# An added 16-row load at the head of SyncE's queue in an add-and-GELU kernel

## The chip, the cores and the metric

The kernel runs on one core of a Trainium2 chip. The metric is the device time of one execution in microseconds; lower is better. Before the change it is 120.06 us (median of three runs, 120.06 to 120.14). All times given as positions ("at 31.45") are microseconds from the start of the profiled span.

## The reference

```python
batch, dim = 1024, 4096          # x and y: float32

def reference(x, y):
    z = x + y
    return (0.5 * z * (1 + np.tanh(np.sqrt(2 / np.pi) * (z + 0.044715 * z ** 3)))).astype(np.float32)
```

It is an elementwise add followed by GELU in its tanh form. Two arrays of 16.78 MB are read and one of 16.78 MB is written; nothing is used twice.

## The kernel before

**Tiling.** Each array is viewed as 128 partitions by 32768 elements; a partition's row is 128 KB of consecutive memory. One tile `z` holds a whole array (128 x 32768). x is loaded straight into it, y is added to it, and the result is written over it and stored from it. y goes through two buffers of 8192 columns each (`YS`), used in turn.

**Transfers.** All are issued by SyncE, in the order of the list `sp` (line 173): y0, x0, y1, x1, y2, y3, and then three stores. A y load has 8192 columns (4 MB in all, 32 KB per partition), an x load 16384 (8 MB), and the stores have 16384, 10240 and 6144. The loads y2 and y3 take over the buffers of y0 and y1, so each waits until the adds that read the old content are done (`needs`, line 183). The first store also waits for the first part of chunk 8's last step (`FIRST`, line 98), so that stores join the queue shortly before the loads end.

**Compute.** The columns are worked on in 16 chunks of 2048 (`CH`). For each chunk: `add` (z += y, on VectorE for six chunks and on GpSimd for ten, table `by_dve`), `mag` (ScalarE writes the absolute value of z into a PSUM tile w), `gelu` (ScalarE applies GELU to -w in place), and `end` (VectorE writes max(z, 0) + w back to z). This uses that GELU(z) is max(z, 0) plus GELU of minus the absolute value of z.

**Order.** Each engine has a list of its own (`sp`, `pool`, `acts`, `dve`). The loop at line 199 emits from each list whatever has its needs emitted already, and the schedule is kept as emitted. What an instruction really waits for at run time are semaphores that the framework derives from the tiles that it reads and writes.

**Head and tail.** `begin_early` (line 9) runs on the finished program: it takes the first `count` transfers of SyncE out of the body, checks that they wait for nothing, and puts them at the front of the program's head, before the start-up work and the barrier that ends it. It is called with a count of 2 (line 214), so y0 and x0 are issued there. `wait_late` (line 23) takes the wait for the last store out of the closing sequence and puts it at the very end, on ScalarE, so that the closing barriers and semaphore clearing run while the last stores are under way.

Of the kernel before, what the change touches and what calls it, by code (L numbers as in the profile page):

```python
# [66 lines left out]
def kernel(  # L67
# [14 lines left out]
    nc = tc.nc  # L82
    P = nc.NUM_PARTITIONS
    fp32 = mybir.dt.float32
# [6 lines left out]
    xv, yv, ov = (a.rearrange("(p n) d -> p (n d)", p=P) for a in (x, y, out))  # L91
# [22 lines left out]
    pool_sb = ctx.enter_context(tc.tile_pool(name="xz", bufs=1))  # L114
# [55 lines left out]
            ends.setdefault(c, ins.ins)  # L170


    sp = [(load_y, 0), (load_x, 0), (load_y, 1), (load_x, 1), (load_y, 2), (load_y, 3)]
    sp += [(store, i) for i in range(len(stores))]
    pool = [(add, c) for c in range(C) if c not in by_dve]
    dve, acts = [], []
    for c in range(C):
        dve += [(add, k) for k in sorted(by_dve) if by_dve[k] == c] + [(end, c)]
        acts += [(mag, c), (gelu, c)]

    needs = {
        load_x: lambda i: [],
        load_y: lambda i: [
            (add, c) for c in over(cr, yr[i][0] - 2 * YS, yr[i][1] - 2 * YS)
# [61 lines left out]
```

## Time and profile before

| what | us |
|---|---|
| median of three runs | 120.06 |
| profiled span, first to last instruction | 118.57 |
| VectorE busy | 59.8 |
| ScalarE busy | 60.8 |
| GpSimd busy | 55.5 |
| last landing of y0 (issued at 0.00) | 12.01 |
| last landing of x0 (issued at 0.43) | 31.35 |
| last landing of y3 | 79.86 |
| first store issued | 77.61 |
| last store issued | 107.56 |
| last landing of the last store | 118.53 |

The profiled execution is one run of its own; its span counts from the first instruction to the last, and the median of the runs lies 1.49 us above it.

How to read it: "busy" counts compute instructions; an instruction that only starts a transfer shows with its engine's queue (SPq for SyncE), and the transfer itself is carried by 16 DMA engines that work next to each other. Each packet of a transfer (here one partition's row) has a record with its start and duration. A load has landed when all 16 engines have reported on its semaphore. The rows and stretches themselves are shown with the prediction.

### The profile page before, as it was taken

Reading aid. Unit: us, or ns where it says so; the run is one execution under the profiler, and the core shown is the slowest. Engines: PE = TensorE matmul, PEld = TensorE weight load, DVE = VectorE, ACT = ScalarE, POOL = GpSimd, SP = SyncE. Lnnn points to the kernel's source line nnn. Section 1 sums busy time; section 2 is a strip of 40 time slices with the busy share of each in tenths; the row PEclk is TensorE's granted clock in tenths of the full one; section 3 lists DMA queues with packets and bytes.
Section 4 is the critical chain, followed back from the end, with each engine's and each line's share of the span. In section 5 each row is a group of like instructions: output and inputs, shape, how many; then the busy total and the mean of one; then the engine's idle time right before and its main releaser. Section 6 shows DMA issues by size and latency. Waiting matters only on the chain.

```text
span 118.6 us, 160 instructions
## 1 busy us (share of the span) xinstructions
DVE 59.8 (50%) x24; ACT 60.8 (51%) x34; POOL 55.5 (47%) x14
## 2 busy tenths in 40 slices
DVE  0000000000399999699994594257999457742000
ACT  5000000000067979999379705797798999940000
POOL 0000000000399999997000029999999999100000
DMA  7989888998889988988899898998899889999996
GB/s 243 464 365 696 354 354 354 663 398 354 354 387 497 531 354 354 707 354 354 354 420 464 365 520 354 531 531 354 354 531 531 354 354 442 442 442 442 398 398 265
DMA packets 1296, 50.33 MB, mean 424 GB/s; under 512 B 144, under 2 KB 144, under 8 KB 144
## 3 DMA queue, kind: packets, MB, share of 16 engines
q1 hardware_dynamic: 1296, 50.33, 98.6%
HBM read 33.55 MB, written 16.78 MB: 424 GB/s over the span
## 4 chain that ended last, share of the span: by engine, by line
DMA 48%; POOL 34%; POOLq 4%; ACT 3%; DVE 2%; issue 0%; SPq 0%; DVEq 0%
POOL z L149 34%; DMA z<-in_x_dram 26%; DMA y<-in_y_dram 21%; POOLq L213 4%; DVE z L166 2%; ACT w L154 2%; ACT w L157 2%; SPq L132 0%; POOLq L149 0%; DVEq L166 0%
## 5 line engine op out<-in xcount | busy, mean ns | idle before, releaser
L149 POOL TENSOR_TENSOR z<-z,y 128x2048 f32<-128x2048 f32 x10 | 55.3, 5563 | 45.6 <-DMA z<-in_x_dram 31.1
L154 ACT ACTIVATE w<-z 128x2048 f32<-128x2048 f32 x16 | 30.1, 1880 | 42.5 <-DVE z L149 36.0
L166 DVE SCALAR_TENSOR_TENSOR z<-z,w 128x2048 f32<-128x2048 f32 (+1 forms) x17 | 36.4, 2157 | 16.0 <-ACT w L157 16.0
L149 DVE TENSOR_TENSOR z<-z,y 128x2048 f32<-128x2048 f32 x6 | 24.0, 4009 | 30.3 <-DMA z<-in_x_dram 30.1
L157 ACT ACTIVATE w<-w 128x2048 f32<-128x2048 f32 x16 | 29.8, 1862 | 0.5
L198 ACT ACT_TABLE_LOAD x1 | 1.3, 1283 | 1.3 <-PEq L230 1.3
L197 DVE MEMSET one<- 128x1 f32 x1 | 0.1, 59 | 1.3 <-PEq L230 1.3
L198 ACT ACTIVATE one<-one 128x1 f32<-128x1 f32 x1 | 0.2, 203 | 0.0
L230 POOL MEMSET const-float32-0.0<- 128x1 f32 x1 | 0.1, 98 | 0.2 <-issue 0.2
L230 POOL MEMSET const-bfloat16-1.0<- 128x1 bf16 x1 | 0.1, 101 | 0.0
L230 POOL MEMSET const-uint8-127<- 128x1 uint8 x1 | 0.1, 101 | 0.0
L230 POOL MEMSET const-float32-1.0<- 128x1 f32 x1 | 0.1, 98 | 0.0
## 6 DMA issues: line engine op xcount, KB each, us to landing
y<-in_y_dram SPq DMA_DIRECT2D x4, 4096.0 KB, 23.7
out_dram<-z SPq DMA_DIRECT2D x1, 5120.0 KB, 14.9
out_dram<-z SPq DMA_DIRECT2D x1, 3072.0 KB, 11.0
z<-in_x_dram SPq DMA_DIRECT2D x2, 44.9
out_dram<-z SPq DMA_DIRECT2D x1, 21.6
```

Source lines behind the costliest of these rows:

```text
L149: eng.tensor_add(out=zt[:, a:b], in0=zt[:, a:b], in1=yt[s][:, o : o + b - a])
L154: nc.scalar.activation(out=wt[c], in_=zt[:, a:b], func=act.Abs)
L157: nc.scalar.activation(out=wt[c], in_=wt[c], func=act.Gelu_apprx_tanh, scale=-1.0)
L166: ins = nc.vector.scalar_tensor_tensor(out=zt[:, a + o : a + o + n], in0=zt[:, a + o : a + o + n], scalar=0.0, in1=wt[c][:, o : o + n], op ...
L197: nc.vector.memset(one, 0.0)
L198: nc.scalar.activation(out=one, in_=one, func=act.Gelu_apprx_tanh)
L213: tc.compile()
L230: nc = _bacc.Bacc("TRN2", target_bir_lowering=False, num_devices=1)
```

## The change

A further entry, `first`, stands at the head of SyncE's list. It allocates a tile of its own, `tiny`, of 128 x 128 float32 (512 B per partition) in the pool that holds `z`, and loads 16 rows of 128 elements of y into it, 512 B each, 8 KB in all. Nothing reads that tile. It has no needs. All else, the count of 2 given to `begin_early` among it, is as before.

```diff
-    sp = [(load_y, 0), (load_x, 0), (load_y, 1), (load_x, 1), (load_y, 2), (load_y, 3)]
+    def first(_):
+        tiny = pool_sb.tile([P, 128], fp32, tag="tiny", name="tiny")
+        nc.sync.dma_start(out=tiny[:16], in_=yv[:16, :128])
+
+    sp = [(first, 0), (load_y, 0), (load_x, 0), (load_y, 1), (load_x, 1), (load_y, 2), (load_y, 3)]
     sp += [(store, i) for i in range(len(stores))]
...
     needs = {
+        first: lambda i: [],
         load_x: lambda i: [],
```

## The prediction

> **What bounds the kernel now.** I first read the page's utilisation rows: is any engine, or the memory traffic, full from end to end?
>
> ```profile
> span 118.6 us, 160 instructions
> DVE 59.8 (50%) x24; ACT 60.8 (51%) x34; POOL 55.5 (47%) x14
> ...
> DMA packets 1296, 50.33 MB, mean 424 GB/s; under 512 B 144, under 2 KB 144, under 8 KB 144
> q1 hardware_dynamic: 1296, 50.33, 98.6%
> ```
>
> No compute engine is busy for more than half of the span; the 16 DMA engines have a packet in hand for 98.6% of it. The chain of waits says something else at first sight:
>
> ```profile
> DMA 48%; POOL 34%; POOLq 4%; ACT 3%; DVE 2%; issue 0%; SPq 0%; DVEq 0%
> ```
>
> The 34% on POOL are adds that run while the queue still has transfers in it: the chain follows back from the last compute instruction, which ends at 107.5, while data flow until 118. So I asked next where in the span the traffic is not full, in stretches (the last two columns are the busy share of the DMA engines and GB/s; a packet counts in the stretch in which it starts, hence shares a little over 1):
>
> ```profile
> 0.00:1.00 1.00, 0.00 (x0) 0.00 (x0) 0.20 (x4) 1.00 0.00 0
> 1.00:4.00 3.00, 0.06 (x1) 1.49 (x2) 0.00 (x0) 1.00 0.98 360
> 4.00:40.00 36.00, 8.55 (x2) 5.61 (x3) 8.51 (x2) 1.00 1.01 436
> 40.00:80.00 40.00, 30.49 (x14) 30.76 (x18) 25.45 (x5) 1.00 1.03 446
> 80.00:116.00 36.00, 20.73 (x8) 22.97 (x13) 21.34 (x5) 1.00 0.96 416
> 116.00:118.60 2.60, 0.00 (x0) 0.00 (x0) 0.00 (x0) 1.00 0.66 284
> ```
>
> Between 4 and 116 us there is no hole. I strung the trace's packet records into 16 chains, one per DMA engine: none has an idle gap over 25 ns, at the seams between the nine transfers either. Each chain carries 3.146 MB, and a 32 KB packet takes 1.21 us (27.1 GB/s; 16 engines 433 GB/s), so a chain needs 3.146 MB / 27.1 GB/s = 116.1 us. The last packets end at 117.75 to 118.07, the last landing is at 118.53, and the span ends at 118.57. So **the time is the moment at which data start to flow, plus 116.1, plus 0.5 of landing**. Only the first term can move, apart from bytes. It stands here:
>
> ```profile
> 0.00 0.38 SPq L132 DMA_DIRECT2D y<-in_y_dram  x1
> 0.43 0.42 SPq L125 DMA_DIRECT2D z<-in_x_dram  x1
> 1.26 0.33 SPq L132 DMA_DIRECT2D y<-in_y_dram  x1
> 1.64 0.45 SPq L125 DMA_DIRECT2D z<-in_x_dram  x1
> ```
>
> SyncE begins the issue of y0 at 0.00 and ends it at 0.38. The packet records begin 0.64 later: the 16 engines' first packets start at 1.02, one after another, the last at 1.95. They take 2.14 us (earliest starter) down to 1.21 (the two latest), against 1.21 for any later packet, and end at 2.77 to 3.17. Taking 1.21 off each end gives the moment at which each engine flows: 1.56 to 1.95.
>
> **The change, part by part.**
>
> *The new issue on SyncE.* One issue of a kind with the four y loads, whose rows show 0.33 to 0.38 us. It is now the first instruction, so it should take the 0.38; y0's issue then starts at 0.43, as x0's does now, and takes 0.33. It ends at 0.76 instead of 0.38: **+0.38 us** on the path, with nothing in front of it to hide it.
>
> *What the DMA engines do with it.* 16 rows of 512 B are 8 KB, against 50.33 MB. If each engine gets one row, that is 512 B / 27.1 GB/s = 0.02 us, and a completion record of 9 ns (the duration of each of the 144 four-byte packets): 0.03 us per engine. These lie in the 0.38 by which y0 comes later, so I count nothing; if that cover is gone, 0.03. If one engine gets all the rows it is 0.3 us on that engine, which would outlast the cover only if the small transfer were itself late.
>
> *The latency of a first transfer.* The trace shows one start from idle and no second, so it does not say whether a small transfer in front takes over part of the start-up of y0. Bounds from the rows: y0's packets can start 0.64 after its issue ends, at 0.76 + 0.64 = 1.40, instead of 1.02. At best all 16 flow at once from 1.40: the last engine gains 1.95 - 1.40 = 0.55. At worst the writing out of a transfer over the 16 engines takes the 0.93 us between first and last start (1.95 - 1.02) whatever its size, and y0's begins behind the small one's: +0.93. I take the spread as it is, shifted by 0.38, because the two engines that start last (1.90 and 1.95) run their first packet at full rate, 1.21: what they wait for is their turn, not data, and they are among the latest to flow, so their turn sets the end.
>
> *What the change moves.* The helper that lifts transfers to the front of the program takes the first two SyncE transfers. Those are now the small load and y0; x0 stays behind in the body. The body's first issue is at 1.26 now, so x0 is issued at about 1.26, y1 at 1.26 + 0.42 + 0.05 = 1.73 and x1 near 2.1. None is needed before y0's last packet ends (the chains show 11.6). I cost this at nothing; the 9.7 us of y0's own packets hide it, and without that cover x0's delay, 1.26 - 0.43 = 0.83, would be paid in full.
>
> *Completion counters.* The landing records show eight counters for nine transfers, y0's used again by the last store. With ten, the last two stores use the small load's and y0's, which have long landed when the stores are issued. The final wait follows the last store's counter; clearing the others may take one more GpSimd instruction, near 112 us, behind which there are 6 us of stores. Nothing.
>
> *What is late next.* Adds, activations and ends follow the landings, so they shift with the stream. The tightest seam is the first store: issued at 77.61 when y3's last landing is at 79.86. It hangs on y2's landing, which shifts by the same amount, so the 2.2 us stay. The last store is issued at 107.56 with the store before it landing at 111.26: 3.7 us.
>
> **Rule against row.** The Trainium skill, "DMA: Bandwidth & Descriptors", in "Rules for kernel authors", speaks against the change: a transfer under 64 KB is mostly overhead and should be merged; its section "Anatomy of one DMA — SWDGE (gpsimd) path" puts the fixed part near 2.0 us, for GpSimd's path, not SyncE's. Paid in series that would give 120.06 + 2.0 = 122.06. The chains' seams here show no such price between transfers that are queued one behind another (no gap over 25 ns), so I do not pay it.
>
> **The sum.** Span 118.57 + 0.38 = 118.95. The median of the runs, 120.06, stands 1.49 above the profiled span, and the change touches nothing outside the span: 120.06 + 0.38 = **120.44 us**. This case's own range is 120.30 (0.14 of the shift absorbed) to 120.55 (issue at x0's 0.43, plus the 0.03 of bytes, and 0.03 more).
>
> **The rivals.**
>
> 1. *The small load warms the path (faster).* Place: the first packet of each engine. It speaks for this that 14 of 16 first packets take longer than 1.21, by up to 0.92: early starters wait for something that happens once. If that and the uneven starts belong to the first touch, and not to y0's size, y0's packets, queued at 1.40, flow on every engine by 1.56, the earliest flow seen now: 1.95 - 1.56 = 0.39 off, 119.67; at the bound of 0.55, 119.51. It decides when the last engine flows before 1.71, that is, ends its first y0 packet before 2.92. Against it: the two latest starters show no such excess, and y0 cannot be queued before 1.40.
> 2. *The delay is hidden by the start-up (no change).* Each engine spends its start-up on the small load, and y0's packets are already queued behind it: the flow starts at 1.56 to 1.95 as now, plus 0.03 of bytes: 120.09. For it: the flow now lags the first starts by up to 0.92, more than the 0.38. Against it: as in 1, the latest starters have no lag to hide in.
> 3. *Writing out is serial with a fixed price (slower still).* +0.93, 120.99. For it: first starts nearly evenly spaced, 0.06 apart. Against it: 0.93 us for 16 rows would mean that the size of a transfer does not count.
> 4. *The change doesn't do what it says*, that is, y0 is left in the body. The helper takes the first two SyncE transfers in program order, and y0 is the second, so I give this no chance of its own; y0 at 1.26 would cost 1.26 us, 121.32.
>
> **How the numbers follow.** My forecast has 0.50, rival 1 0.24, rival 2 0.18, rival 3 (with all dearer mishaps) 0.08. A difference of 0.2% (0.24 us) is about what a measurement of this kernel can tell from no change. Slower by more than that: forecast and rival 3, 0.58; within it: rival 2, 0.18; faster: 0.24. The predicted time is the forecast's 120.44. The range reaches down over rival 1's central value to 119.65, and up to 120.75, a third of the way from the forecast's upper end toward rival 3's value; below lies a third of rival 1 (0.08), above all of rival 3 (0.08).
>
> **What would show it.** Right: a small issue of about 0.38 at 0.00, y0's issue from 0.43 to 0.76, y0's first packets starting at 1.4 to 2.3, its landing near 12.4 instead of 12.0, and the gap-free chains after it 0.38 later up to a span of 118.95. The spread step is wrong if y0's first packets all end within a few tenths of 2.9, or if y0 lands at 12.0 or before. The cover of x0 is wrong if a gap opens between y0's last packet and x0's first. The whole reading is wrong if the time moves by more than 0.93 with y0's landing unmoved: then something after the start, such as the first store's issue, has come to matter.

## The result and the profile after

The changed kernel takes 120.68 us (median of 17 runs, 120.48 to 121.17) beside 120.16 us for the kernel before on the same chips (17 runs): a ratio of 1.0044, 95% interval 1.0033 to 1.0055, which is 0.53 us of 120.16. It is slower, by a little more than the 0.38 us forecast. The time lies in the stated range of 119.65 to 120.75, though above the forecast's own 120.30 to 120.55.

The utilisation rows of the changed kernel's page; the stretches below have the same columns as before the change:

```profile
span 119.6 us, 161 instructions
DVE 59.8 (50%) x24; ACT 60.8 (51%) x34; POOL 55.5 (46%) x14
...
DMA packets 1329, 50.34 MB, mean 421 GB/s; under 512 B 161, under 2 KB 177, under 8 KB 177
q1 hardware_dynamic: 1328, 50.34, 98.4%
...
DMA 47%; POOL 33%; POOLq 4%; ACT 3%; DVE 2%; issue 0%; DVEq 0%
```

32 packets more than before (16 of 512 B, 16 of completion) and one of another queue; the busy times of the compute engines and the chain's shares are the old ones.

```profile
0.00:1.00 1.00, 0.00 (x0) 0.00 (x0) 0.20 (x4) 1.00 0.00 0
1.00:4.00 3.00, 0.06 (x1) 1.49 (x2) 0.00 (x0) 1.00 1.04 352
4.00:40.00 36.00, 8.03 (x2) 5.09 (x3) 7.99 (x2) 1.00 1.01 437
40.00:80.00 40.00, 30.99 (x14) 30.22 (x18) 24.90 (x5) 1.00 0.99 419
80.00:116.00 36.00, 20.74 (x8) 24.03 (x13) 22.40 (x5) 1.00 1.00 433
116.00:119.60 3.60, 0.00 (x0) 0.00 (x0) 0.00 (x0) 1.00 0.76 328
```

The queue is full as before. Two things differ: the head, and the stretch from 40 to 80, where packets of 419 GB/s started instead of 446 (packets count where they start, so part of that difference lies at the stretch's ends). The head first, in SyncE's timeline (start, duration, engine, line, instruction):

```profile
0.00 0.38 SPq L175 DMA_DIRECT2D tiny<-in_y_dram  x1
0.44 0.41 SPq L132 DMA_DIRECT2D y<-in_y_dram  x1
1.25 0.33 SPq L125 DMA_DIRECT2D z<-in_x_dram  x1
1.63 0.42 SPq L132 DMA_DIRECT2D y<-in_y_dram  x1
2.11 0.48 SPq L125 DMA_DIRECT2D z<-in_x_dram  x1
```

The small load takes y0's place, and y0's issue ends at 0.85 instead of 0.38: 0.47 later. x0 has moved into the body, as foreseen. By the packet records the small load's packets run from 1.01 to 1.42, and y0's 16 first packets now start at 1.48 to 2.02 (before: 1.02 to 1.95) and end at 3.29 to 3.69 (before: 2.77 to 3.17). y0 has landed at 12.52 instead of 12.01, x0 at 31.87 instead of 31.35: +0.51 each, and it stays so up to y1 (41.58 against 41.08).

This profiled execution is 1.06 us longer than the one before, twice what the medians show. The rest arises in the stretch from 40 to 80: x1 lands 19.81 us after y1 instead of 19.36, because many of its 64 KB packets took 2.49 to 2.59 us instead of 2.42. Whether that belongs to the change is a question for the experiments.

### The profile page after: what moved, and what is told of

It is laid out like the page before. It is cut to its first block, busy times and chain, and to the rows that moved or that the text cites. A ratio compares the mean times of both kernels' runs of the same rounds, so it can differ in the third digit from the quotient of the medians.

```text
span 119.6 us, 161 instructions
## 1 busy us (share of the span) xinstructions
DVE 59.8 (50%) x24; ACT 60.8 (51%) x34; POOL 55.5 (46%) x14
## 4 chain that ended last, share of the span: by engine, by line
DMA 47%; POOL 33%; POOLq 4%; ACT 3%; DVE 2%; issue 0%; DVEq 0%
POOL z L149 33%; DMA z<-in_x_dram 26%; DMA y<-in_y_dram 22%; POOLq L218 4%; DVE z L166 2%; ACT w L154 2%; ACT w L157 2%; POOLq L149 0%; DVEq L166 0%
```

## The experiments

The theory: the stream starts a fixed time after y0's issue on SyncE ends, nothing later can catch up, and so the loss is the issue time put in front. The rivals: the DMA engines charge a price for a small transfer; the price is paid once; leaving x0 in the body costs something. Each kernel was timed against the kernel before on the same chip. The ratio compares means, so the losses given in us, which are worked out from it, can differ a little from the differences of the medians. The diffs are against the changed kernel where the small load is kept, and against the kernel before where it is dropped. "Issue end" and "flow" are read in its own trace: the end of y0's issue on SyncE, and the moment at which the last of the 16 engines flows (the end of its first y0 packet, less 1.21 us). Not in the table, since it hardly varies: y0's earliest packet starts 0.63 to 0.64 us after the issue's end in all twelve profiles.

| kernel | median us | ratio to before, 95% interval | issue end | flow | flow less issue end |
|---|---|---|---|---|---|
| before | | | 0.38 | 1.95 | 1.57 |
| changed | 120.68 | 1.0044 (1.0033 to 1.0055) | 0.85 | 2.48 | 1.63 |
| changed, again | 120.71 | 1.0048 (1.0031 to 1.0065) | 0.86 | 2.44 | 1.57 |
| changed, third time | 120.78 | 1.0054 (1.0034 to 1.0074) | 0.87 | 2.49 | 1.62 |
| two small loads in front | 121.05 | 1.0080 (1.0067 to 1.0093) | 1.31 | 2.97 | 1.66 |
| small load of one row | 120.52 | 1.0040 (1.0028 to 1.0052) | 0.75 | 2.46 | 1.71 |
| small load, y0 and x0 lifted | 120.55 | 1.0037 (1.0024 to 1.0050) | 0.86 | 2.51 | 1.65 |
| the same again | 120.58 | 1.0039 (1.0026 to 1.0052) | 0.85 | 2.60 | 1.75 |
| small load second, x0 in the body | 120.20 | 1.0011 (0.9999 to 1.0024) | 0.37 | 1.94 | 1.57 |
| small load second, x0 lifted | 120.18 | 1.0010 (0.9992 to 1.0027) | 0.37 | 1.99 | 1.62 |
| small load issued by ScalarE | 120.15 | 1.0004 (0.9994 to 1.0013) | 0.37 | 1.98 | 1.61 |
| before, x0 in the body | 120.18 | 1.0012 (1.0000 to 1.0024) | 0.38 | 2.07 | 1.69 |

### Two small loads

```diff
-        tiny = pool_sb.tile([P, 128], fp32, tag="tiny", name="tiny")
-        nc.sync.dma_start(out=tiny[:16], in_=yv[:16, :128])
+        for n in ("tiny", "tiny2"):
+            t = pool_sb.tile([P, 128], fp32, tag=n, name=n)
+            nc.sync.dma_start(out=t[:16], in_=yv[:16, :128])
...
-    begin_early(nc, 2)
+    begin_early(nc, 3)
```

> Two small loads with a tile each are issued ahead of y0, all three lifted to the head. Theory (each issue on SyncE costs its own 0.38 to 0.46): y0's issue ends near 1.25 instead of 0.85, +0.85 to +1.05 us over the kernel before, twice the loss of one. Rival (a price paid once, by the first touch of the engines or by whatever transfer comes second): +0.5 us as with one. Rival (serial writing out, 0.93 each): +1.5 or more.

Measured: ratio 1.0080, +0.96 us, nearly twice the loss of one. SyncE's timeline:

```profile
0.00 0.85 SPq L176 DMA_DIRECT2D tiny<-in_y_dram  x2
0.89 0.42 SPq L132 DMA_DIRECT2D y<-in_y_dram  x1
```

Two issues take 0.85 us, y0's ends at 1.31, 0.93 after the 0.38 of the kernel before, and the time follows it. The price is neither paid once (+0.5 expected) nor 0.93 for each load (+1.5 or more expected).

### One row instead of 16

```diff
-        nc.sync.dma_start(out=tiny[:16], in_=yv[:16, :128])
+        nc.sync.dma_start(out=tiny[:1], in_=yv[:1, :128])
```

> The small load has 1 row of 512 B instead of 16, so that a single DMA engine has work from it. Theory (the price is SyncE's issue, not the 16 engines' share): +0.4 to +0.55 us over the kernel before, as with 16 rows. Rival (the loss comes from handing the small transfer to 16 engines): under +0.2 us, with y0's first packets earlier than 1.3.

Measured: ratio 1.0040, +0.48 us. SyncE's timeline:

```profile
0.00 0.34 SPq L175 DMA_DIRECT2D tiny<-in_y_dram  x1
0.39 0.35 SPq L132 DMA_DIRECT2D y<-in_y_dram  x1
```

The packet records hold a single 512 B packet, so one engine alone has work from it, yet the loss is within 0.05 us of that with 16 rows. What the other 15 engines do with the small load is not the price. y0's issue ends 0.10 sooner here than in the changed kernel, at 0.75, and y0's earliest packet starts sooner with it (1.38 instead of 1.48), but the last engine flows at 2.46, no sooner than there (2.48). So the flow follows the end of the issue only to within some 0.1 us.

### The small load from ScalarE's queue

```diff
-        nc.sync.dma_start(out=tiny[:16], in_=yv[:16, :128])
+        nc.scalar.dma_start(out=tiny[:16], in_=yv[:16, :128])
...
-    moved = [i for i in body if i.engine == SP and isinstance(i, mybir.InstDMACopy)][:count]
+    for eng, n in ((mybir.EngineType.SP, count), (mybir.EngineType.Activation, 1)):
+        moved = [i for i in body if i.engine == eng and isinstance(i, mybir.InstDMACopy)][:n]
```

> The small load of 16 rows is issued by ScalarE, at the head of its own queue, so that SyncE's first issue is y0 again at 0.00 while the same small transfer still runs beside it. Theory (SyncE's issue time is the price): within 0.1 us of the kernel before, y0's first packets from about 1.02. Rival (the small transfer's passage through the DMA engines or the descriptor writing delays y0): +0.3 us or more. Rival (warming): at least 0.2 us faster than before, all of y0's first packets ending before 2.95.

Measured: ratio 1.0004, +0.05 us, with an interval (0.9994 to 1.0013) that includes 1. The timeline of that kernel, both queues:

```profile
0.00 0.37 SPq L132 DMA_DIRECT2D y<-in_y_dram  x1
0.12 0.38 ACTq L175 DMA_DIRECT2D tiny<-in_y_dram  x1
0.42 0.42 SPq L125 DMA_DIRECT2D z<-in_x_dram  x1
```

The same transfer, issued in the same half microsecond, costs nothing measurable once it is off SyncE's queue. It brings nothing either, though it is no test of warming: its packets come only at 2.92 to 3.20, after each engine's first packet of y0. For the same reason this run alone doesn't separate the small load's issue from its packets. The packet records do: in the changed kernel the small load's packets are over at 1.42 and y0's earliest starts at 1.48, as long after its own issue as in the kernel before. No run delayed y0's issue without a transfer in front.

### The small load behind y0

```diff
-    sp = [(first, 0), (load_y, 0), (load_x, 0), (load_y, 1), (load_x, 1), (load_y, 2), (load_y, 3)]
+    sp = [(load_y, 0), (first, 0), (load_x, 0), (load_y, 1), (load_x, 1), (load_y, 2), (load_y, 3)]
```

> The small load is issued second, between y0 and x0. Theory (only what stands in front of y0's issue counts): within 0.05 us of the kernel before, y0's first packets from 1.02 and its last landing at 12.0; the seam behind y0 grows by no more than 0.05. Rival (a small transfer costs the DMA engines a fixed price wherever it stands): +0.4 us or more, as a gap of that length between y0's last packets and x0's first.

Measured: ratio 1.0011, interval from 0.9999. The +0.13 us is above the 0.05 expected and below the 0.4 of the rival. SyncE's timeline:

```profile
0.00 0.37 SPq L132 DMA_DIRECT2D y<-in_y_dram  x1
0.43 0.42 SPq L175 DMA_DIRECT2D tiny<-in_y_dram  x1
1.25 0.34 SPq L125 DMA_DIRECT2D z<-in_x_dram  x1
```

y0 stands first and its issue ends at 0.37 again. At the seam itself only the small load's own 0.03 us per engine is added: the packet chains show no gap over 3 ns between y0's last packet, the small one and x0's first, and x0 lands at 31.36 (before: 31.35). I ran it again with x0 lifted as well (a count of 3):

> y0, then the small load, then x0, all three lifted to the head. Theory (what is queued behind y0 is free): within 0.08 us of the kernel before. Rival (the +0.13 of the kernel with the small load second came from the small load's passage at the seam): +0.1 us or more again. If it falls to nothing here, that +0.13 belongs to x0's late issue or to scatter.

Measured: 1.0010, interval from 0.9992 to 1.0027. That is +0.12 us (the medians differ by 0.09), on the rival's side of its line at 0.1, with an interval (-0.10 to 0.32) that holds the theory's 0.08 as well. In its profile x0 lands 19.36 us after y0 (before: 19.34) and the span is 118.59 (before: 118.57). A price for a small load behind y0, if there is one, is near 0.1 us and does not show at the seam.

### x0 back in the head

```diff
-    begin_early(nc, 2)
+    begin_early(nc, 3)
```

> The small load, y0 and x0 all go to the head of the program (three transfers are lifted instead of two). Theory (the delay of y0's issue is the whole loss, and x0's later issue is hidden under y0's 9.7 us of packets): as the changed kernel, +0.4 to +0.55 us over the kernel before, y0's last landing near 12.5, no gap between y0 and x0. Rival (x0, left behind in the body, costs something): less than +0.25 us, and y0's landing stays at 12.5 while x0's comes earlier than 31.87 by 0.2 or more.

Measured: ratio 1.0037, +0.44 us; y0 lands at 12.52 and x0 at 31.87, both as in the changed kernel. But the median lay 0.13 us below the changed kernel's, so I repeated both, the changed kernel twice:

> The changed kernel unchanged, for a second profile. Theory: +0.4 to +0.55 us; y0's landing near 12.5, and the interval between the landings of y1 and x1 back at about 19.35 as in the kernel before (it was 19.81 in the changed kernel's first profile, which I take for this one execution's). Rival (the longer interval belongs to the change): 19.7 to 19.9 again.

> As the earlier kernel with three transfers lifted (small load, y0, x0), beside the changed kernel on the same chip. Theory (x0's later issue is free): the same as the changed kernel within 0.08 us, both +0.4 to +0.55 over the kernel before. Rival (leaving x0 to the body costs some 0.1 to 0.15 us, as the two medians 120.55 and 120.68 hint): 0.1 us or more below the changed kernel again.

> The changed kernel, beside the one with three transfers lifted. Theory: within 0.08 us of it. Rival: 0.1 us or more above it. If its profile shows stretches of slow packets again (x packets over 2.45 us or 32 KB packets over 1.25 us in the middle of the span) and the other's does not, the rival gains.

Measured: 1.0048, 1.0039 and 1.0054. Over all runs the changed kernel has a median of 120.71 (32 runs), the one with x0 lifted 120.57 (16 runs): 0.14 us. Side by side in one batch they stand at 120.78 (8 runs) and 120.58 (11 runs), which is the 0.1 us or more of the rival, but the intervals of their ratios overlap. To see x0's place alone, I ran the kernel before without any small load, but with x0 left in the body:

> The kernel before without any small load, but with only y0 lifted to the head, so that x0 is left in the body as the change leaves it. Theory (x0's later issue is free under y0's packets): within 0.08 us of the kernel before, y0's landing at 12.0 and x0's at 31.35. Rival (it costs the 0.15 us by which the changed kernel lies above the one with three transfers lifted, through slow load packets between 30 and 80 us): +0.1 to +0.2 us, with a wider scatter of the runs.

Measured: ratio 1.0012, interval from 1.0000 to 1.0024. That is +0.14 us, within the rival's range, and the runs scatter a little more (to 120.69 against 120.53); but the interval reaches nothing, and the medians differ by 0.08. SyncE's timeline of that kernel:

```profile
0.00 0.38 SPq L132 DMA_DIRECT2D y<-in_y_dram  x1
0.79 0.33 SPq L125 DMA_DIRECT2D z<-in_x_dram  x1
```

x0 is issued at 0.79 instead of 0.43, and 1.25 in the changed kernel; at the seam behind y0 that costs nothing (x0 lands 19.33 us after y0 here, 19.35 in the changed kernel, 19.34 before). What remains is the scatter. Summed over each profiled execution, what load packets between 30 and 80 us took beyond their usual time is 0.75 us per engine in the changed kernel's first profile, 0.4 in its second, 0.1 in its third, and 0.7 in the one with the small load second; it is at most 0.15 in all others of the table except the two small loads (about 0.25). All four that stand out leave x0 in the body, and none of the table's five profiles with x0 lifted stands out; but three others with x0 in the body (the one-row kernel, the changed kernel's third, and this one) don't either. So the longer y1-to-x1 interval of the first profile does not come with the change each time, since the second and third profiles have 19.35 there. And with the small load second, the loss is the same with x0 in the body (0.13) and lifted (0.12). **Whether x0's late issue makes such stretches likelier, at 0.1 us or so in the median, stays open.**

### Two attempts at an earlier start

My prediction had the last engines' turn in the handing out set the flow. If so, handing out less per queue should bring it forward. Both kernels drop the small load and issue y0 as two transfers, one from SyncE and one from ScalarE (lifted as above, in place of the list's own load of y0). By partitions:

```diff
...
+        nc.sync.dma_start(out=yt[0][:64], in_=yv[:64, :YS])
+        nc.scalar.dma_start(out=yt[0][64:], in_=yv[64:, :YS])
...
```

> No small load; y0 is issued as two transfers of 64 partitions, one by SyncE and one by ScalarE at the same time at the head of both queues. Theory (what sets the start is the issue and then the turn of each of the 16 engines, so half as many rows each to hand out in parallel brings the last engine forward): up to 0.3 us faster than the kernel before, y0's last first-packet end before 3.0. Rival (the first packets wait for data, not for their turn): no change within 0.1 us, first packets ending at 2.8 to 3.2 as before; or slower, if two rings on each engine get in each other's way, visible as packets of y0 well over 1.21 us each.

Measured: 130.02 us, ratio 1.0822 (1.0802 to 1.0842). A miss by far; the sign that the second rival named, y0's packets well over 1.21 us each, is there, at a size that none expected. The stretches of that kernel:

```profile
4.00:12.00 8.00, 0.00 (x0) 0.00 (x0) 0.00 (x0) 1.00 1.00 217
...
40.00:80.00 40.00, 34.38 (x12) 29.58 (x16) 24.23 (x4) 1.00 1.00 433
```

The DMA engines are busy throughout, yet move 217 GB/s, half of the 433 later on: y0's packets take about 2.4 us instead of 1.21. y0's 128 packets on 16 engines are eight for each, so that is some 9.5 us, nearly the whole loss of 9.9. The two issues take 0.54 us each, against 0.38 for y0's before. With such a price it tells nothing of the start. By columns, each transfer over all 128 partitions:

```diff
...
+        nc.sync.dma_start(out=yt[0][:, : YS // 2], in_=yv[:, : YS // 2])
+        nc.scalar.dma_start(out=yt[0][:, YS // 2 :], in_=yv[:, YS // 2 : YS])
...
```

> No small load; y0 is issued as two transfers of 128 partitions by 4096 columns, one by SyncE and one by ScalarE at the same time, so that every engine gets its first 16 KB packet from whichever queue reaches it first, and both write to all partitions. Theory (an engine's turn in the handing out sets the last start): up to 0.3 us faster than before, the last first-packet flow before 1.75. Rival (first packets wait for data, whatever their turn): within 0.1 us of the kernel before. Rival (two issues at once hold each other up): issues of 0.5 us or more each and a loss of 0.1 to 0.3 us.

Measured: 120.35 us, ratio 1.0015 (1.0000 to 1.0030), +0.18 us (the medians differ by 0.26). The heads of both queues in that kernel:

```profile
0.00 0.38 SPq L175 DMA_DIRECT2D y<-in_y_dram  x1
...
0.12 0.37 ACTq L176 DMA_DIRECT2D y<-in_y_dram  x1
```

The two issues run side by side at the usual duration, so here they don't hold each other up. First packets, now of 16 KB, start at 1.00 to 1.45 and take 0.93 to 1.38 us, against 0.61 for later ones: by them the last engine flows at 2.53 - 0.61 = 1.92, as before the change (1.95), though the last start came 0.5 earlier. All 16 first packets came from SyncE's queue, none from ScalarE's. But some of the second packets were slow too (up to 1.14 us). Over the first two packets, the same 32 KB as one packet before, the last engine ends at 3.43 instead of 3.17, and x0 lands at 31.64 instead of 31.35. So the earlier starts brought no earlier flow; it came some 0.26 us later, which is where the loss lies. Neither kernel beats the one before.

## Why the prediction was right, and where it was not

**The bound.** Right: the time is the start of the flow, plus a stream without gaps. Across the kernels of the table the issue end moves from 0.37 to 1.31, and the flow follows 1.57 to 1.75 us after it. From y0's last landing to the last store's it is 106.46 to 106.54 us in nine of the twelve profiles; the other three (106.79, 107.07 and 107.11) are those with most time in slow packets. So a late start is not won back.

**The sum.** The term for the issue was mis-sized. I let the small load take the 0.38 of a first issue (it did) and gave y0's issue 0.33, that of the body's y issue. It took 0.41. In these kernels an issue's duration goes by its place more than by what it loads: the second in the head takes 0.41 to 0.42 when it is x0 (before), y0 (changed) or the small load (second place), except 0.35 behind the one-row load; the first in the body takes 0.33 to 0.35, y or x. (The 0.54 of the 64-partition halves doesn't fit this and is not explained.) So the issue term is 0.85 - 0.38 = +0.47, and the measured loss of 0.53 (0.40 to 0.66 by its interval) holds that, but not the 0.38. Of the 0.24 us between the forecast's 120.44 and the measured 120.68, some 0.09 is this term and 0.10 the starting point: the kernel before stands at 120.16 over 17 runs, not at the 120.06 of three. The time lies above the forecast's own range, and only the widening toward rival 3 takes it in. Its upper end is miscounted as well: a third of the way from 120.55 to 120.99 is 120.70, not 120.75. The margin to that is 0.02 us, and the repeats' medians (120.71 and 120.78) lie above it. With a shift that was over a quarter too small, it is part luck that the time lies in the range.

**The start-up step.** The shift was right and its reason was not. I took the two latest starters as waiting for their turn, and their turn as what sets the end. The rows that I had speak against it: the earliest starter, at 1.02 with 2.14 us, ends at 3.15, only 0.01 before the latest starter's end. Nor are the starts nearly evenly spaced; the distances go from 0.002 to 0.22 us. In nine of the twelve profiles the last engine to flow is not the last to start. The last start differs between kernels whose y0 issue ends at the same time: 1.95 in the kernel before, 1.49 with the small load second, and the last engine flows at 1.95 and 1.94. With the starts brought forward by the column halves the flow came no sooner. So what sets the flow lies between a packet's start and its data, 1.57 to 1.75 us after the issue's end in all twelve profiles; what it is, no run shows.

**Rivals.** Warming is refuted as far as the small load could warm anything: its packets start on all 16 engines at 1.01 to 1.39 and have landed by 1.70, and y0's first packets still take 1.67 to 2.02. Hiding the delay in the start-up is refuted by the same rows: the lag of 1.6 begins anew with y0's issue. The fixed price of 0.93 per transfer is refuted by the two small loads, which cost 0.96 together. The overhead rule of the Trainium skill, "DMA: Bandwidth & Descriptors", "Rules for kernel authors", is not a price in series here: the chains pass a small transfer inside a full queue with no gap over 3 ns, and what is paid at the head is the issue.

**What I costed at nothing.** The bytes and x0's move: nothing at the seam but the 0.03 us of bytes, as forecast; a possible 0.1 us from x0's move is left open above. The late work moved with the stream: the first adds start at 31.97 and 32.01 instead of 31.45 and 31.49 (the changed kernel's timeline, with what ended the wait),

```profile
31.97 8.80 DVE L149 TENSOR_TENSOR z<-z,y 128x2048 f32<-128x2048 f32 x2 [30.58 <-DMA z<-in_x_dram]
32.01 6.61 POOL L149 TENSOR_TENSOR z<-z,y 128x2048 f32<-128x2048 f32 x1 [31.57 <-DMA z<-in_x_dram]
```

and the stores' leads are kept (first store issued at 78.67 with y3's landing at 80.94).

## What to carry to other kernels

In a kernel whose transfer queue never runs dry, the issue of the first large transfer should be the first instruction of its queue: one issue ahead of it cost 0.44 to 0.65 us here in six comparisons (0.36 to 0.48 of it by the end of y0's issue), as much for a single 512 B row as for 8 KB, and nothing later won that back. A small load that has to be early goes behind the first large one, or on another queue, where it measured 0.05 to 0.13 us, in no run clearly above nothing. Where a helper takes "the first n" transfers, an insertion moves the cut too; check what fell behind it.

## What the runs showed of the hardware that was not expected

- Two transfers of 64 partitions each, on two queues, moved 217 GB/s together, where 128-partition transfers moved 433; the kernel lost 9.9 us by it. The Trainium skill, "DMA: Bandwidth & Descriptors", "Rules for kernel authors", says that such halves serialize on the same engines and are not worth it; that row gives no rate. The trace agrees: at nearly every moment all 16 engines carry packets of one queue, and so of one half of the partitions, two packets each before they change over. Two queues as such are not the cause: the column halves, on the same two queues over 128 partitions, ran 16 KB packets at the full 0.61 us. So the 64 partitions are what is left, though no run loaded 64 partitions from one queue.
- A transfer on ScalarE's queue, issued 0.12 us after y0's, got no packet in until each engine had finished its first packet of y0: the small load's packets start at 2.92 to 3.20, and it lands at 4.79 instead of 1.70.
- The first packets' extra time, 0.3 to 0.9 us in most (0.46 to 0.81 in the changed kernel, up to 0.92 before), does not go away when a small transfer has just run on the same engines and queue, and it is there for 16 KB packets as for 32 KB ones.
